# Grouped attention on one core: fresh tiles for score slots and output banks, other waits, and a plan with other constants

## The chip, the core and the metric

The kernel runs on one core of a Trainium2 chip. Five engines of the core take part, each with its own stream of instructions: TensorE (PE) multiplies matrices into PSUM, VectorE (DVE) and ScalarE (ACT) work on elements, GpSimd (POOL) and SyncE (SP) here mostly issue transfers (DMA). [...]The metric is device time of one execution in microseconds (us): 372.54 us before the change, the median of three runs (372.14 to 372.68).

## What is computed

Attention with 8 query heads that share 2 key/value heads in groups of four; batch 8, sequence 1024, head dimension 64:

```python
# q: (8, 8, 1024, 64), k and v: (8, 2, 1024, 64), all float32
for g in range(2):
    q_group = q[:, 4 * g : 4 * g + 4]          # four query heads of one group
    scores = (1 / sqrt(64)) * q_group @ k[:, g:g+1].transpose(0, 1, 3, 2)
    attn = exp(scores - max(scores, axis=-1))
    attn = attn / (sum(attn, axis=-1) + 1e-8)
    output[:, 4 * g : 4 * g + 4] = attn @ v[:, g:g+1]
```

The kernel calls one pair of batch and query head a job: 64 jobs. The 1024 keys of a job are cut into 8 chunks of 128 keys, so there are 512 chunks of scores of 128 x 1024 numbers each, each of which needs an exponential. The maximum is not subtracted (the scores are small); the sum of a row comes out of the second product, since v has a column of ones beside it.

## The kernel before

TensorE writes a chunk of scores into one of three slots in PSUM (`sps[0..2]`, two banks each). A slot is emptied in one of two ways. ScalarE takes most chunks, with one exponential each. VectorE takes about a quarter and builds an exponential out of bits: a first pass (`yt`, out of the slot) turns the score into a 16-bit integer that, read as bfloat16, is a power of two with a linear mantissa; three more operations, over two chunks at once, split it into two numbers `et` and `zt` whose sum is the exponential. The second product takes both, which makes two matmuls instead of one for each piece of such a chunk.

```python
elif kind == "score":
    for half in range(2):
        now = nc.tensor.matmul(sps[x][:, half, :], lhsT=..., rhs=..., start=True, stop=True)
elif kind == "act":
    p = pp.tile([128, 2, HS], BF16, name="pt")
    nc.scalar.activation(out=p, in_=sps[x], func=AF.Exp, scale=scale)
elif kind == "dpass":
    nc.vector.tensor_scalar(out=yt[ch][:, i, :, :], in0=sps[x], scalar1=EXP_A, scalar2=EXP_B,
                            op0=ALU.mult, op1=ALU.add)
# "zh":  zt = (yt & 0x7F) | 0x3F00      "two": et = yt & 0x7F80      "mul": zt = yt * zt
elif kind == "pv":        # second product into one of two output banks: 7 pieces of 128 rows per bank
    nc.tensor.matmul(ops[plan.group_of[x] % 2][...], lhsT=p[...], rhs=va[...], ...)
elif kind == "pvl":       # the same for the last job, chunk by chunk, into a score slot that is spare by then
    ...
elif kind in ("rec", "norm"):   # VectorE: reciprocal of the row sums, then multiply into ost
    ...
elif kind == "store":     # DMA of one job's 1024 rows out of ost, a ring of 56 pieces
    ...
```

In which order all this is issued is decided ahead of time, in Python, by a class `Plan`. It steps through the clocks of TensorE, ScalarE and VectorE with constants for the length of each operation and for the hand-over between engines, and writes down the list of events from which the instructions are then issued. A few of the constants (in ns) and the rule for a score that is meant for ScalarE:

```python
M_PAIR = 226      # the two score matmuls of a chunk
M_PTAIL = 45      # from there to the exponential that reads them
M_ACT = 905       # an exponential
M_GAP = 120; M_RUNWAY = 1300; M_BACK = 3000; M_WAIT = 150; GRAIN = 4
...
runway = tA - t + M_ACT * len(aq)
slack = runway - cold * M_PAIR - M_PTAIL - (M_SWITCH if mode != "s" else 0)
...
if slack <= M_GAP or (full and runway < M_RUNWAY):
    kind = "A"            # now a score for ScalarE; otherwise second products, GRAIN matmuls at a time
```

`M_BACK` is the amount of pending work under which VectorE is given another chunk. The tile framework puts in the semaphore waits from what each operation reads and writes. Each `sps[i]` and `ops[i]` is one tile for the whole kernel.

At the start, k and q of the first job are loaded as float32, cast, transposed by TensorE into slot 2 (k in its first half, q in its second) and copied out:

```python
nc.sync.dma_start(out=f32["k"], in_=rows(k[0, 0]))       # rows: "(c p two) d -> p c (two d)", 512-byte runs
nc.scalar.dma_start(out=f32["q"], in_=rows(q[0, 0]))
...
nc.vector.tensor_copy(out=k0[:, 0, 0:128], in_=turned["k"][:, 0:128])
nc.scalar.activation(out=qt[0][:, 0, 0:256], in_=turned["q"][:, 0:256], func=AF.Copy)
nc.vector.tensor_copy(out=qt[0][:, 0, 256:HS], in_=turned["q"][:, 256:HS])
nc.vector.tensor_copy(out=k0[:, 0, 128:HS], in_=turned["k"][:, 128:HS])
```

Of the kernel before, what the change touches and what calls it, by code (L numbers as in the profile page):

```python
# [9 lines left out]

M_START = 5150
M_SWAP = 700
M_Q1 = 3500
# [5 lines left out]
M_PAIR = 226  # L19
M_PTAIL = 45  # L20
M_SWITCH = 92
M_MM = 33.5
# [3 lines left out]
M_FIX = 76  # L26
# [5 lines left out]
M_REC = 115  # L32
M_GAP = 120
M_RUNWAY = 1300
M_BACK = 3000
M_WAIT = 150
STEP = 10
INF = float("inf")
PB = 7
NPIECE = 8  # L40
GRAIN = 4
MXD = 2
STEPS = (("zh", M_D4), ("two", M_D4), ("mul", M_D2))


class Plan:


    def __init__(self, nj, npt, nct, nyt):
        self.nj, self.npt, self.nct, self.nyt = nj, npt, nct, nyt  # L50
        self.ev = []
        self.on_d = set()
        self.spare = None
        self.mms = [8] * nj

        self.last = (nj - 1) * NPIECE
        self.groups = [(i, min(i + PB, self.last)) for i in range(0, self.last, PB)]
        self.groups += [(self.last, self.last + 4), (self.last + 4, self.last + 8)]
        self.group_of = [g for g, (lo, hi) in enumerate(self.groups) for _ in range(lo, hi)]
        self.run()  # L60

    def run(self):
# [3 lines left out]
        qready = [M_START] + [M_START + M_Q1 + M_QSTEP * j for j in range(nj - 1)]  # L66
        slot_free = [M_START, M_START, M_START + M_SWAP]
        aq, dq = [], []
# [14 lines left out]
        a = 0  # L83

        def pick_d():
            for j in range(a, min(nj, a + 3)):
                if todo[j] and dcount[j] < MXD and qready[j] <= tP:
                    return j
            if a == nj - 1 and len(todo[a]) > 2 and dcount[a] < MXD + 1:
                return a  # L90
            return None

        while pc < last or steps or norms:
# [12 lines left out]
            if tD == t:  # L106
                end = None
                if dq and dq[0][0] <= t:
                    _, s, j, c = dq.pop(0)
                    if open_chain is None:  # L110
                        open_chain = dict(id=nch, pairs=[], at=0)
                        ch_left[nch] = set()
                        nch += 1
                        used_c += 1
# [16 lines left out]
                else:  # L131
# [4 lines left out]
                    for ch in chains:  # L136

                        late = dlast == (ch["id"], 0) and ch["at"] == 0
                        key = (late, 3 - ch["at"], ch)
                        if best is None or key[:2] < best[:2]:  # L140
                            best = key
                    if best:
                        at = max(t, dend + M_DEP) if best[0] else t
                        ch = best[2]
                        if ch is None:
                            _, _, lo, hi = norms.pop(0)
                            ev.append((t, "norm", (lo, hi), None, None))
                            end = at + M_FIX + 64 * (hi - lo) * M_D1
                            out_free[group_of[lo] % 2] = end + M_DTAIL + M_SEE
                            dlast = None  # L150
                        else:
                            n = len(ch["pairs"])
                            kind, rate = STEPS[ch["at"]]
                            ev.append((t, kind, None, ch["id"], n))
                            end = at + M_FIX + 1024 * n * rate
                            ch["at"] += 1
                            dlast = (ch["id"], ch["at"])
                            if ch["at"] == len(STEPS):
                                chains.remove(ch)
                                for j, c in ch["pairs"]:  # L160
                                    p_ready[j][c] = end + M_DTAIL + M_SEE
# [12 lines left out]
            if not dq and len(chains) < self.nyt and (open_chain or used_c < self.nct):  # L174
                back = max(tD - t, 0)
                for ch in chains:
                    n = len(ch["pairs"])
                    back += sum(M_FIX + 1024 * n * r for _, r in STEPS[ch["at"] :])
                if back < M_BACK:
                    dj = pick_d()  # L180
# [11 lines left out]
            if kind:  # L192
# [13 lines left out]
                else:  # L206
                    dcount[j] += 1
                    self.mms[j] += 1
                    self.on_d.add((j, c))
            elif (  # L210
# [33 lines left out]
            elif (  # L244
# [14 lines left out]
                ev.append((tP, "pvl", c, len(steps), None))  # L259
                tP += NPIECE * M_MM * (2 if (nj - 1, c) in self.on_d else 1)  # L260
                if not steps:
# [18 lines left out]
def kernel(  # L280
# [42 lines left out]
    rp = ctx.enter_context(tc.tile_pool(name="rp", bufs=4))  # L323
    psum = ctx.enter_context(tc.tile_pool(name="psum", bufs=1, space=bass.MemoryType.PSUM))

    ctx.enter_context(tc.manual_schedule())

    sps = [psum.tile([128, 2, HS], FP32, name=f"sp{i}") for i in range(3)]
    ops = [psum.tile([128, 512], FP32, name=f"ops{i}") for i in range(2)]
    RING = PB * NPIECE  # L330
# [17 lines left out]
    def cast_k(b, g):  # L348
# [5 lines left out]
        )  # L354

    def load_v(b, g):
        t = vsp.tile([128, NH, 2 * D], FP32, name="vs")
        vs[(b, g)] = t
        return nc.sync.dma_start(
            out=t, in_=v[b, g].rearrange("(c p two) d -> p c (two d)", p=128, two=2)  # L360
        )

# [28 lines left out]

    def rows(x):
        return x.rearrange("(c p two) d -> p c (two d)", p=128, two=2)

    f32 = {x: kvp.tile([128, NH, 2 * D], FP32, name=f"{x}32") for x in "kq"}
    b16 = {x: kvp.tile([128, NH, 2 * D], BF16, name=f"{x}16") for x in "kq"}
    kt[(0, 0)] = ktp.tile([128, 2, HS], BF16, name="kt")
    qt[0] = qp.tile([128, 1, HS], BF16, name="qt")
    nc.sync.dma_start(out=f32["k"], in_=rows(k[0, 0]))
    nc.scalar.dma_start(out=f32["q"], in_=rows(q[0, 0]))  # L400
    load_v(0, 0)
    cast_q(1)
    make_identity(nc, ident)
    cast_q(2)

    def dummy(n, cols):
# [7 lines left out]
    nc.scalar.activation(out=b16["q"], in_=f32["q"], func=AF.Copy)  # L414
    turned = {"k": sps[2][:, 0, :], "q": sps[2][:, 1, :]}
    for x in "kq":
# [13 lines left out]
    nc.vector.tensor_copy(out=k0[:, 0, 0:128], in_=turned["k"][:, 0:128])  # L430
    nc.scalar.activation(out=qt[0][:, 0, 0:256], in_=turned["q"][:, 0:256], func=AF.Copy)
    nc.vector.tensor_copy(out=qt[0][:, 0, 256:HS], in_=turned["q"][:, 256:HS])  # L432
    nc.vector.tensor_copy(out=k0[:, 0, 128:HS], in_=turned["k"][:, 128:HS])
# [29 lines left out]
    pt, yt, et, zt, where = {}, {}, {}, {}, {}  # L463
    now = None

    def terms(j, par):

        for ci in range(NC):
            c = ci if par == 0 else (ci + NH) % NC
            if (j, c) in where:  # L470
                ch, i = where[(j, c)]
                yield ci, et[ch].bitcast(BF16)[:, i, par, :]
                yield ci, zt[ch].bitcast(BF16)[:, i, par, :]
            elif (j, c) in pt:
                yield ci, pt[(j, c)][:, par, :]

    for _, kind, x, j, c in ev:
        if kind in ("ck", "cq"):
# [13 lines left out]
        elif kind == "score":  # L492
            b, h = divmod(j, H)
            t = kt[(b, h // HPG)]

            for half in range(2):
# [9 lines left out]
        elif kind == "act":  # L506
            p = pp.tile([128, 2, HS], BF16, name="pt")
            pt[(j, c)] = p
            nc.scalar.activation(out=p, in_=sps[x], func=AF.Exp, scale=scale)  # L509
        elif kind == "dpass":  # L510
            ch, i = j
            where[c] = j
            if i == 0:
                yt[ch] = yp.tile([128, 2, 2, HS], U16, name="yt")
            nc.vector.tensor_scalar(  # L515
                out=yt[ch][:, i, :, :], in0=sps[x],
                scalar1=EXP_A, scalar2=EXP_B, op0=ALU.mult, op1=ALU.add,
# [8 lines left out]
        elif kind == "two":  # L526

            et[j] = ep.tile([128, 2, 2, HS], U16, name="et")
            nc.vector.tensor_scalar(  # L529
                out=et[j][:, 0:c], in0=yt[j][:, 0:c], scalar1=0x7F80, scalar2=None,  # L530
                op0=ALU.bitwise_and,
            )
        elif kind == "mul":
            z = zt[j].bitcast(BF16)[:, 0:c]
            nc.vector.tensor_tensor(  # L535
                out=z, in0=yt[j].bitcast(BF16)[:, 0:c], in1=z, op=ALU.mult
            )
        elif kind == "pv":
# [3 lines left out]
            lo = x % PB * (D + 1)  # L542
            every = list(terms(job, par))
            for i in range(j, j + c):
                ci, p = every[i]
# [9 lines left out]
        elif kind == "pvl":  # L555
            b, h = divmod(NJ - 1, H)
            first = j == NC - 1
            for i in range(NPIECE):
                par = i % 2
# [13 lines left out]
        elif kind == "half":  # L573
# [3 lines left out]
            (nc.scalar if i else nc.sync).dma_start(  # L577
                out=out[b, h].rearrange("(s p two) d -> p s (two d)", p=128, two=2)[:, i : i + 2],
                in_=ost[:, lo % RING : lo % RING + 4, :].rearrange("p (s two) d -> p s (two d)", two=2),
# [19 lines left out]
        elif kind == "store":  # L599
            b, h = divmod(j, H)  # L600
            r = j * NPIECE % RING
            nc.sync.dma_start(
                out=out[b, h].rearrange("(s p two) d -> p s (two d)", p=128, two=2),
                in_=ost[:, r : r + NPIECE, :].rearrange("p (s two) d -> p s (two d)", two=2),
            )


# [28 lines left out]
```

## Time and profile before

| what | us |
|---|---|
| time, median of 3 | 372.54 |
| span of the profiled execution, first to last instruction | 370.2 |
| first exponential starts | 7.95 |
| last exponential starts / ends | 362.23 / 363.26 |
| last matmul ends | 366.04 |
| ScalarE, VectorE, TensorE busy | 356.5, 354.1, 349.7 |

A line of a group reads: line of the kernel, engine, operation, what it writes and reads with shapes, count; then busy time and the mean length of one in ns; then the idle time of the engine just ahead of these operations, and who ended it. Busy time counts overlapping records once. A line of the timeline reads: start and length in us, engine, line, operation, count, and in brackets the idle time ahead of it and who ended that. A line of the table of waits reads: who waited for whom, us in total, how often, the longest.

### The profile page before, as it was taken

To read this page: it belongs to the slowest core of one execution; us is meant where nothing else is said; L and a number is where in the kernel's file an instruction comes from. 1 tells how busy PE (TensorE), PEld (TensorE's weight loads), DVE (VectorE), ACT (ScalarE), POOL (GpSimd) and SP (SyncE) were. 2 spreads that over 40 slices of the span, in tenths; PEclk is the share of its full clock that TensorE was granted. 3 is DMA by queue.
4 is the path that set the end of the run, shared out by engine and by line. 5 is a ranking of instruction groups with operands and counts; after the bars stand their busy time and mean duration, and the time that the engine had idled before them with its cause. 6 is when DMAs were issued, how large, how long until landed. Compare 5 with 4: busy or idle time off the path is not lost.

```text
span 370.2 us, 14248 instructions
## 1 busy us (share of the span) xinstructions
PE 349.7 (94%) x6199; PEld 222.7 (60%) x6199; DVE 354.1 (96%) x479; ACT 356.5 (96%) x386; POOL 50.6 (14%) x100
## 2 busy tenths in 40 slices
PE   6899999999999999999999999999999999999995
PEld 2465666666565666666566666656666656666655
DVE  3999999999999999999999999999999999999995
ACT  3999999999999999999999999999999999999992
POOL 4002021011212011021111112102011111201000
PEclk9999999999999999999999999999999999999999
DMA  7446756865757674776566577466576756775223
GB/s 178 78 88 106 157 121 101 151 136 130 125 113 132 118 159 86 147 139 120 104 140 133 122 133 119 114 158 115 107 154 96 155 97 143 122 143 98 60 58 87
DMA packets 90702, 44.83 MB, mean 121 GB/s; under 512 B 45488, under 2 KB 89392, under 8 KB 89392
## 3 DMA queue, kind: packets, MB, share of 16 engines
q1 hardware_dynamic: 87344, 33.31, 39.1%
q0 software_dynamic: 2496, 10.23, 20.5%
q8 instruction: 48, 0.79, 1.0%
q10 hardware_dynamic: 800, 0.39, 0.4%
q14 instruction: 14, 0.11, 0.2%
HBM read 25.17 MB, written 27.00 MB: 141 GB/s over the span
## 4 chain that ended last, share of the span: by engine, by line
ACT 39%; DVE 24%; PE 24%; issue 10%; DMA 2%; DVEq 0%; ACTq 0%
ACT pt L509 39%; DVE yt L515 13%; PE ops L546 12%; PE sp L499 11%; DVE zt L535 4%; DVE zt L522 2%; DVE et L529 2%; DVE ost L593 2%; DMA qt<-qd 1%; DMA k<-in_k_dram 1%; PE sp L565 1%; DVE rec L590 1%; PE sp L418 0%; DVE k L413 0%; DVE qt L432 0%
## 5 line engine op out<-in xcount | busy, mean ns | idle before, releaser
L509 ACT ACTIVATE pt<-sp 128x1024 bf16<-128x1024 f32 x383 | 354.2, 1054 | 2.2 <-PE sp L499 1.6
L499 PE MATMUL sp<-qt,kt 64*128 64x512 bf16 x1024 | 172.0, 384 | 13.3 <-ACT pt L509 6.2
L546 PE MATMUL ops<-va,pt 128*128 128x65 bf16 x3024 | 176.8, 194 | 0.0
L515 DVE TENSOR_SCALAR yt<-sp 128x1024 uint16<-128x1024 f32 x129 | 157.1, 1218 | 6.1 <-PE sp L499 4.8
L546 PEld LDWEIGHTS <-pt 128*128 128x128 bf16 x3024 | 129.2, 97 | 52.6 <-issue 52.6
L546 PE MATMUL ops<-va,et 128*128 128x65 bf16 x1008 | 120.4, 194 | 0.0
L546 PE MATMUL ops<-va,zt 128*128 128x65 bf16 x1008 | 119.5, 194 | 0.9 <-DVE zt L535 0.6
L546 PEld LDWEIGHTS <-et 128*128 128x128 bf16 x1008 | 79.6, 98 | 28.4 <-issue 26.2
L546 PEld LDWEIGHTS <-zt 128*128 128x128 bf16 x1008 | 80.3, 97 | 2.4 <-DVE zt L535 1.5
L535 DVE TENSOR_TENSOR zt<-yt,zt 128x2048 bf16<-128x2048 bf16 (+1 forms) x65 | 80.5, 1238 | 0.0
L499 PEld LDWEIGHTS <-kt 64*128 64x128 bf16 x1024 | 47.9, 93 | 53.4 <-issue 31.7
L343 POOL DMA_DIRECT2D qd<-in_q_dram x63 | 32.9, 522 | 223.8 <-PE sp L499 212.8
L529 DVE TENSOR_SCALAR et<-yt 128x2048 uint16<-128x2048 uint16 (+1 forms) x65 | 44.8, 690 | 0.0
L593 DVE TENSOR_TENSOR ost<-ops,rec 128x448 f32<-128x448 f32 x72 | 44.2, 614 | 0.0
L522 DVE TENSOR_SCALAR zt<-yt 128x2048 uint16<-128x2048 uint16 (+1 forms) x65 | 44.0, 677 | 0.0
L351 POOL DMA_DIRECT2D kd<-in_k_dram x15 | 7.3, 488 | 59.4 <-PE sp L499 51.2
L590 DVE RECIPROCAL rec<-ops 128x7 f32<-128x7 f32 x72 | 14.1, 196 | 0.0
L364 POOL CAST va<-vs 128x512 bf16<-128x512 f32 x16 | 10.2, 638 | 2.4 <-DMA vs<-in_v_dram 2.4
L408 PE MATMUL ops<-warm 128*128 128x128 bf16 (+1 forms) x31 | 5.0, 308 | 1.2 <-DVE warm L335 1.2
L408 PEld LDWEIGHTS <-warm 128*128 128x128 bf16 x31 | 2.2, 108 | 4.2 <-issue 3.0
L413 DVE CAST k<-k 128x512 bf16<-128x512 f32 x1 | 0.4, 429 | 2.6 <-DMA k<-in_k_dram 2.6
L414 ACT ACTIVATE q<-q 128x512 bf16<-128x512 f32 x1 | 0.6, 629 | 2.2 <-DMA q<-in_q_dram 2.2
(28 smaller groups left out, 18.6 us busy)
## 6 DMA issues: line engine op xcount, KB each, us to landing
out_dram<-ost SPq DMA_DIRECT2D x63, 256.0 KB, 2.8
qd<-in_q_dram POOLq DMA_DIRECT2D x63, 128.0 KB, 3.5
vs<-in_v_dram SPq DMA_DIRECT2D x16, 256.0 KB, 4.2
kd<-in_k_dram POOLq DMA_DIRECT2D x15, 128.0 KB, 3.2
kt<-kt SPq DMA_DIRECT2D x30, 64.0 KB, 3.6
qt<-qd SPq DMA_TRANSPOSE x63, 3.8
k<-in_k_dram SPq DMA_DIRECT2D x1, 256.0 KB, 3.6
q<-in_q_dram ACTq DMA_DIRECT2D x1, 256.0 KB, 4.0
```

Source lines behind the costliest of these rows:

```text
L343: return nc.gpsimd.dma_start(out=t.rearrange("(a x) d -> a (x d)", x=4), in_=q[b, h].rearrange("(a x) d -> a (x d)", x=8),)
L351: return nc.gpsimd.dma_start(out=t.rearrange("(a x) d -> a (x d)", x=4), in_=k[b, g].rearrange("(a x) d -> a (x d)", x=8),)
L364: return nc.gpsimd.tensor_copy(out=va[:, b * G + g, :, :, 0:D], in_=vs.pop((b, g)).rearrange("p c (two d) -> p c two d", two=2),)
L499: now = nc.tensor.matmul(sps[x][:, half, :], lhsT=t[lo : lo + D, c // NH, ci % NH * 128 : (ci % NH + 1) * 128], rhs=qt[j][lo : lo + D, 0, ...
L509: nc.scalar.activation(out=p, in_=sps[x], func=AF.Exp, scale=scale)
L515: nc.vector.tensor_scalar(out=yt[ch][:, i, :, :], in0=sps[x], scalar1=EXP_A, scalar2=EXP_B, op0=ALU.mult, op1=ALU.add,)
L522: nc.vector.tensor_scalar(out=zt[j][:, 0:c], in0=yt[j][:, 0:c], scalar1=0x7F, scalar2=0x3F00, op0=ALU.bitwise_and, op1=ALU.bitwise_or,)
L529: nc.vector.tensor_scalar(out=et[j][:, 0:c], in0=yt[j][:, 0:c], scalar1=0x7F80, scalar2=None, op0=ALU.bitwise_and,)
L535: nc.vector.tensor_tensor(out=z, in0=yt[j].bitcast(BF16)[:, 0:c], in1=z, op=ALU.mult)
L546: nc.tensor.matmul(ops[plan.group_of[x] % 2][:, lo : lo + D + 1], lhsT=p[:, qs * 128 : (qs + 1) * 128], rhs=va[:, b * G + h // HPG, ci % N ...
L590: nc.vector.reciprocal(out=rec[:, 0:n], in_=o[:, :, D])
L593: nc.vector.tensor_tensor(out=ost[:, r : r + n, :], in0=o[:, :, 0:D], in1=rec[:, 0:n].unsqueeze(2).to_broadcast([128, n, D]), op=ALU.mult,)
```

## The change

It does six things. Each use of a score slot and of an output bank becomes a tile of its own, in a pool with one buffer per slot, so that the readers of the slot's earlier contents are waited for by the matmul that writes, and no longer by the operation that reads. Every twelfth exponential is made to depend on the one fifteen before it, so that the others need no wait on their own engine for a buffer written long before. Waits for old stores are put on one of VectorE's three short operations (`two`) and not on the normalisation. The plan's constants are changed, among them the hand-over from scores to their reader (`M_PTAIL`). For the last two jobs VectorE adds `et` and `zt` itself, and the second product takes one matmul per piece. The first k, q and v are loaded, and the first output stored, with runs of 2 KB (another order of the rows, the same for all four), and q is transposed into slot 1 and copied out in one piece.

```diff
-M_START = 5150
-M_SWAP = 700
+M_START = 5450
+M_SWAP = 1200
-M_PTAIL = 45
+M_PTAIL = 205
-M_GAP = 120
-M_RUNWAY = 1300
-M_BACK = 3000
-M_WAIT = 150
+M_GAP = 60
+M_RUNWAY = 1500
+M_BACK = 2500
+M_WAIT = 200
-GRAIN = 4
+GRAIN = 3
-STEPS = (("zh", M_D4), ("two", M_D4), ("mul", M_D2))
+TAIL = 2
+STEPS = (("zh", M_D4), ("two", M_D4), ("mul", M_D2), ("add", M_D2))
... (in the plan: jobs from nj - TAIL on have the fourth step, and no second matmul;
...  the last job's third chunk for VectorE, allowed before, is gone)
-    psum = ctx.enter_context(tc.tile_pool(name="psum", bufs=1, space=bass.MemoryType.PSUM))
+    banks = {
+        x: ctx.enter_context(tc.tile_pool(name=x, bufs=1, space=bass.MemoryType.PSUM))
+        for x in ("sp0", "sp1", "sp2", "op0", "op1")
+    }
-    sps = [psum.tile([128, 2, HS], FP32, name=f"sp{i}") for i in range(3)]
-    ops = [psum.tile([128, 512], FP32, name=f"ops{i}") for i in range(2)]
+    def new_slot(i):
+        sps[i] = banks[f"sp{i}"].tile([128, 2, HS], FP32, name=f"sp{i}")
+        return sps[i]
... (new_bank likewise)
+    def rows(x, fours=False):
+        how = "(p c two) d -> p c (two d)" if fours else "(c p two) d -> p c (two d)"
-    nc.sync.dma_start(out=f32["k"], in_=rows(k[0, 0]))
-    nc.scalar.dma_start(out=f32["q"], in_=rows(q[0, 0]))
+    nc.sync.dma_start(out=f32["k"], in_=rows(k[0, 0], True))
+    nc.scalar.dma_start(out=f32["q"], in_=rows(q[0, 0], True))
-    turned = {"k": sps[2][:, 0, :], "q": sps[2][:, 1, :]}
+    turned = {"k": new_slot(2)[:, 0, :], "q": new_slot(1)[:, 0, :]}
-    nc.scalar.activation(out=qt[0][:, 0, 0:256], in_=turned["q"][:, 0:256], func=AF.Copy)
-    nc.vector.tensor_copy(out=qt[0][:, 0, 256:HS], in_=turned["q"][:, 256:HS])
+    nc.scalar.activation(out=qt[0][:, 0, :], in_=turned["q"], func=AF.Copy)
... (score)
+            where_s[(j, c)] = new_slot(x)
... (act; the first pass likewise reads where_s)
-            nc.scalar.activation(out=p, in_=sps[x], func=AF.Exp, scale=scale)
+            exps.append(nc.scalar.activation(out=p, in_=where_s[(j, c)], func=AF.Exp, scale=scale))
+            if len(exps) % 12 == 0 and len(exps) > 16:
+                tc.add_manual_dep(
+                    exps[-1].ins, exps[-16].ins.name, Sync, reason="buffers written before"
+                )
... (two)
+            while stores and stores[0][0] < when - 10000:
+                tc.add_manual_dep(ins.ins, stores.pop(0)[1].ins.name, Sync, reason="old stores")
+        elif kind == "add":
+            z = zt[j].bitcast(BF16)[:, 0:c]
+            nc.vector.tensor_tensor(
+                out=z, in0=et[j].bitcast(BF16)[:, 0:c], in1=z, op=ALU.add
+            )
```

## The prediction

> **What bounds the kernel now.** I read the page's busy line first, then the costliest groups, the table of waits, and the timeline of the first 8 us and the last 8 us; what the views round away I took from the start and end times of single records of the trace.
>
> The busy line says that no engine is alone at the limit:
>
> ```profile
> PE 349.7 (94%) x6199; PEld 222.7 (60%) x6199; DVE 354.1 (96%) x479; ACT 356.5 (96%) x386; POOL 50.6 (14%) x100
> ```
>
> ScalarE and VectorE both stand at 96%, so a gain has to be had on both. The groups say with what they are filled:
>
> ```profile
> L509 ACT ACTIVATE pt<-sp 128x1024 bf16<-128x1024 f32 x383 | 354.2, 1054 | 2.2 <-PE sp L499 1.6
> L499 PE MATMUL sp<-qt,kt 64*128 64x512 bf16 x1024 | 172.0, 384 | 13.3 <-ACT pt L509 6.2
> L515 DVE TENSOR_SCALAR yt<-sp 128x1024 uint16<-128x1024 f32 x129 | 157.1, 1218 | 6.1 <-PE sp L499 4.8
> ```
>
> 512 score chunks: 383 exponentials on ScalarE, 129 first passes on VectorE. Idle time before the exponentials is only 2.2 us, and that misleads. The records of neighbours overlap (mean 1054 ns, but a new one starts every 904 ns, the median of the 382 distances from start to start), so an exponential that comes 100 or 200 ns late leaves no gap; it only shrinks the overlap. The count shows it: from the first start (7.95 us) to the last (362.23 us) are 354.28 us, and 382 x 0.904 is 345.3 us. So 8.9 us are lost there, a third of it at most visible as a wait. Of these, 7.6 us sit in 67 distances of more than 925 ns, and most of the rest in the exponential after each late one, which typically starts 17 ns later than 904.
>
> Whom the 67 wait for I got by pairing each with its two score matmuls. In all but two the slot had been free for over 100 ns (median 0.36 us) when the scores were started, so TensorE was busy with other work: they were issued too late, not held up by the slot. The exponential starts 428 ns (median) after the start of the second score matmul in the 11 cases where it carries one wait, and 489 ns in the 56 where it carries two. The second wait thus costs some 60 ns, though it is on something long finished.
>
> VectorE shows the same, and here as idle time:
>
> ```profile
> DVE yt L515 <- PE sp L499: 4.8, 15, 0.7
> ```
>
> 32 of its first passes start with over 20 ns of idle time before them, 6.0 us in all; 27 of the 32 carry two waits and start 496 ns after the second score matmul, 5 carry one and start at 419.
>
> The start and the end are the third part:
>
> ```profile
> 4.35 0.43 DVE L413 CAST k<-k 128x512 bf16<-128x512 f32 x1 [2.64 <-DMA k<-in_k_dram]
> 4.75 0.63 ACT L414 ACTIVATE q<-q 128x512 bf16<-128x512 f32 x1 [2.22 <-DMA q<-in_q_dram]
> ...
> 6.41 0.38 ACT L431 ACTIVATE qt<-sp 128x256 bf16<-128x256 f32 x1 [1.03 <-DVE kt L430]
> 6.83 0.42 DVE L432 CAST qt<-sp 128x256 bf16<-128x256 f32 x1 [0.45 <-ACT qt L431]
> ```
>
> ```profile
> 366.13 0.18 DVE L590 RECIPROCAL rec<-sp 128x4 f32<-128x4 f32 x1 [1.31 <-PE sp L565]
> ```
>
> The loads of k and q end the first waits; then q's transpose leaves in two halves one behind the other (6.41 to 7.25 us), the second half on VectorE. At the end the last exponential ends at 363.26 and the last VectorE multiplication at 364.04, but the last 88 matmuls (L565) run until 366.04; two normalisations and the store make it 370.2.
>
> **What the Trainium skill says.** Perfetto Trace Analysis, Identifying Dependency Chains: an instruction that waits for several engines may get EventSemaphore instructions in front of it. The trace agrees, with 279 of them before the exponentials and 68 before the first passes:
>
> ```profile
> L509 ACTq EVENT_SEMAPHORE  x279: 17/17/840, 8.0 to 362.0; - x140
> L515 DVEq EVENT_SEMAPHORE  x68: 21/21/21, 15.9 to 359.1; - x68
> ```
>
> VectorE: DVE Perf Modes, The DRAIN you can't avoid: a semaphore after each operation cost nothing extra there. That agrees for waits already met: the normalisations (L593) with a store's wait in front overlap their predecessor by about 83 ns, those without by about 82. So a wait only costs where its instruction is late. DMA: Bandwidth & Descriptors, Why small descriptors are slow: each DMA operation carries a fixed metadata cost, so fewer and larger pieces are better. The trace of before has 512-byte pieces only in these first loads (27 ns each on its engine); what 2 KB pieces take, no run here shows yet.
>
> **The change part by part.** What is on each engine I counted in the two programs' instruction orders.
>
> *Waits.* Fresh tiles drop the wait for the slot's last reader: 70 exponentials lose a VectorE wait, 68 first passes a ScalarE wait. Self-waits of exponentials fall from 226 to 31. On ScalarE the late ones gain 56 x 60 ns = 3.4 us, capped by how late each was: 7.6 falls to 4.5 us. On VectorE 27 x 77 ns = 2.1 us. The store waits leave the 56 normalisations for 51 operations that mostly had no wait: worth about nothing, by the 83 against 82 ns above.
>
> *Plan.* The hand-over constant grows by 160 ns (45 to 205; with the 226 that the plan counts for a pair this is 431, near the 428 measured), the margin falls by 60: a score for ScalarE is started some 100 ns earlier before it runs dry. Taking 100 ns more off each of the 67 leaves about 1.3 us of the 4.5, with 17 still late. With their followers, and new late ones in a denser plan, I put the loss on ScalarE at 2.5 us instead of 8.9: **-6.4 us**. For VectorE I take 6.0 to about 2.5: -3.5 us.
>
> *Split.* 384 exponentials and 128 first passes: +0.9 us on ScalarE. VectorE loses one pass of 1.14 us and the three short operations of a single chunk (0.34 + 0.34 + 0.60): -2.4 us. Its two adds over 128x2048 cost what the same-sized multiplication does, 1.14 us from start to start: +2.3 us. TensorE loses 40 of 5128 products of probabilities with values, some 1.2 us at about 30 ns, of use only at the end.
>
> *Start.* The 2 KB loads: k landed 3.6 us after issue, q 4.0. 512 pieces at 27 ns over 16 engines are 0.86 us; I guess 0.4 us less for both. q's transpose leaves in one ScalarE operation, which need no longer wait for VectorE's read of the shared slot: 6.1 to 6.75 instead of 6.41 to 7.25 (0.63 us is the 512-wide operation of L414): 0.5 us. First score and first exponential **-0.9 us**.
>
> *End.* In the new order the last job has 64 products, not 88, and behind the last exponential's wait stand 8, some 0.25 us; in before the last product ended 2.8 us behind the last exponential. If VectorE is ready by then: **-2.3 us**. It probably is not far off: before, its last multiplication ended 0.8 us behind the last exponential. From the items above it comes forward by 0.9 + 3.5 + 2.4 - 2.3 = 4.5, to 359.5 us with its last add. In the new order one normalisation more stands behind this add than stood behind the last multiplication (0.53 us from start to start), so 359.0. ScalarE's last exponential: 363.3 - 0.9 + 0.9 - 6.4 = 356.9.
>
> *Sum.* By ScalarE, with 0.4 us to the last product, 1.3 for the normalisations and 2.9 for the store: 356.9 + 4.6 = 361.5. By VectorE: 359.0, then up to 48 products (1.4 us, those that the order puts from the add's chunks on), 1.3 and 2.9: 364.6. The executions took 372.54 against a span of 370.2, so +2.3: 363.8 by one and 366.9 by the other. VectorE's figure rests on the more cautious guess (3.5 of 6.0 us), and the order places the add's products three chunks ahead of the last exponential's, as if the add were done by then, so I lean to ScalarE's and say **364.3 us**, 2.2% less.
>
> **Rivals.** (1) *Latency bound by slots*: with three slots and the score started as soon as it can be, the ring exponential, score, exponential becomes the limit, and earlier issue can't help. Against it: 65 of the 67 late scores found a slot already free; for it: the group of score matmuls shows 6.2 us waiting for ScalarE. Then only the 60 ns count: about 366.8. (2) *VectorE becomes the bound*: its dependent operations keep their stalls and the backlog limit shrinks from 3.0 to 2.5 us, so it may run dry more often. For it: 6.0 us idle today, and the two adds are dependent chains at the very end. About 366 to 368. (3) *Almost no wait left*: waits fall to about 1 us on both, the loads gain 1 us: about 361.5. (4) *TensorE becomes the bound*: 94% busy overlaps itself, and idle time before its scores is 13.3 us, so I give it little; then 368 or more.
>
> **Range and chances.** Rivals 1 and 2 set the upper end, 3 the lower: 361.0 to 367.8. The 2% line is at 365.1, 0.8 us above my number, with an uncertainty of about 2.5 us: **0.6 faster, 0.38 within 2%, 0.02 slower**. All parts point the same way, and slower would need a plan that misses by 14 us.
>
> **What would show it.** Right: EVENT_SEMAPHORE before the exponentials near 31 and before the first passes 0; first exponential near 7.05 us; mean distance of exponentials from 927 to about 911 ns; late ones at 428 ns behind their second score, none at 489; last product within 0.5 us of the last exponential. Wrong: as many late exponentials as before with the slot just released (rival 1); VectorE idle still at 6 us, or L605 waiting for the add at the end (rival 2); k landing no sooner than 3.6 us.

## The result, and the profile after

| what | before | after |
|---|---|---|
| time, median | 372.6 us | 366.81 us (366.55 to 367.96) |
| span of the profiled execution | 370.2 us | 364.9 us |
| exponentials on ScalarE | 383 | 384 |
| first exponential starts | 7.95 us | 7.36 us |
| last exponential ends | 363.26 us | 360.28 us |
| last product ends | 366.03 us | 360.76 us |
| last VectorE operation of a chunk ends | 364.04 us | 356.62 us |

The change makes the kernel faster by 1.5%: ratio 0.9853, 95% interval 0.9831 to 0.9876. That lies inside the range, but the gain is smaller than the 2.2% that I had put in the middle: I had given 0.6 to a gain of more than 2% and 0.38 to one within 2%, and it was within.

The page of after, its busy line and the two groups that empty the slots (in a group: busy time, mean length of one in ns, then idle time ahead of them):

```profile
PE 346.3 (95%) x6155; PEld 220.5 (60%) x6155; DVE 351.6 (96%) x476; ACT 355.1 (97%) x387; POOL 51.3 (14%) x100
...
L532 ACT ACTIVATE pt<-sp 128x1024 bf16<-128x1024 f32 x384 | 352.6, 1099 | 1.0 <-PE sp L522 0.7
...
L543 DVE TENSOR_SCALAR yt<-sp 128x1024 uint16<-128x1024 f32 x128 | 155.8, 1217 | 2.3 <-PE sp L522 2.1
```

Divide busy time by count: 352.6 / 384 = 918 ns for one exponential, where before it was 354.2 / 383 = 925. Records of this group overlap and busy time counts them once. A late exponential that leaves no gap stays in this busy time, so the quotient is the pace plus the delays that the overlap hides, an upper limit of the pace. The distance from one end to the next shows the pace itself: its median is 917 ns in before and in after. The idle time ahead of VectorE's first passes fell from 6.1 to 2.3 us. The waits themselves, counted at the operations, are those that the change was to remove; the first passes have no line of this kind any more:

```profile
L532 ACTq EVENT_SEMAPHORE  x31: 17/17/17, 28.4 to 358.2; - x31
```

The start, from the timeline of after (start and length in us):

```profile
4.33 0.63 ACT L434 ACTIVATE q<-q 128x512 bf16<-128x512 f32 x1 [1.89 <-DMA q<-in_q_dram]
4.51 0.43 DVE L433 CAST k<-k 128x512 bf16<-128x512 f32 x1 [2.80 <-DMA k<-in_k_dram]
...
6.07 0.60 ACT L451 ACTIVATE qt<-sp 128x512 bf16<-128x512 f32 x1 [1.10 <-PE sp L438]
...
7.36 3.99 ACT L532 ACTIVATE pt<-sp 128x1024 bf16<-128x1024 f32 x4 [0.70 <-PE sp L522]
```

q's cast comes 0.42 us sooner than before, k's 0.16 us later; q's copy is one operation and ends at 6.67 us instead of 7.25. The end, VectorE's timeline of after:

```profile
355.39 1.23 DVE L571 TENSOR_TENSOR zt<-et,zt 128x2048 bf16<-128x2048 bf16 x1
356.53 0.62 DVE L633 TENSOR_TENSOR ost<-ops,rec 128x448 f32<-128x448 f32 x1
358.49 0.21 DVE L630 RECIPROCAL rec<-ops 128x7 f32<-128x7 f32 x1 [1.33 <-PE ops L584]
358.73 0.62 DVE L633 TENSOR_TENSOR ost<-ops,rec 128x448 f32<-128x448 f32 x1
360.80 0.18 DVE L630 RECIPROCAL rec<-sp 128x4 f32<-128x4 f32 x1 [1.45 <-PE sp L605]
```

The last add ends at 356.62 us, 3.66 us ahead of the last exponential, and after that VectorE waits for TensorE. Of the two engines that empty the slots, ScalarE is the one that sets the end.

**The ledger of the span.** The parts below are differences of the times in the table and of the count of exponentials; the lost time of ScalarE is the time from the end of the first exponential to the end of the last, less 917 ns for each after the first (why 917 and not the 904 of the prediction is the first experiment):

| part | before | after | difference, us |
|---|---|---|---|
| start of the first exponential | 7.95 | 7.36 | -0.59 |
| the exponentials, 383 and 384: the first 1.02, each other 0.917 | 351.32 | 352.24 | +0.92 |
| lost time between exponentials | 3.99 | 0.68 | -3.31 |
| last exponential to last product | 2.77 | 0.48 | -2.29 |
| last product to the end of the span | 4.17 | 4.11 | -0.06 |
| sum | 370.2 | 364.9 | -5.33 |

### The profile page after: what moved, and what is told of

The parts are those of the page before. It is cut to its first block, busy times and chain, and to the rows that moved or that the text cites. A ratio compares the mean times of both kernels' runs of the same rounds, so it can differ in the third digit from the quotient of the medians.

```text
span 364.9 us, 13795 instructions
## 1 busy us (share of the span) xinstructions
PE 346.3 (95%) x6155; PEld 220.5 (60%) x6155; DVE 351.6 (96%) x476; ACT 355.1 (97%) x387; POOL 51.3 (14%) x100
## 3 DMA queue, kind: packets, MB, share of 16 engines
q0 software_dynamic: 2496, 10.23, 21.3%
## 4 chain that ended last, share of the span: by engine, by line
ACT 56%; DVE 37%; PE 4%; DMA 1%; issue 1%
ACT pt L532 56%; DVE yt L543 16%; DVE zt L566 8%; DVE zt L550 5%; DVE ost L633 4%; DVE et L557 4%; PE sp L522 2%; DMA k<-in_k_dram 1%; DVE rec L630 1%; PE ops L584 1%; PE sp L605 1%; PE sp L438 0%; PE ops L428 0%; ACT qt L451 0%; DVE k L433 0%
## 5 line engine op out<-in xcount | busy, mean ns | idle before, releaser
L532 ACT ACTIVATE pt<-sp 128x1024 bf16<-128x1024 f32 x384 | 352.6, 1099 | 1.0 <-PE sp L522 0.7
L584 PE MATMUL ops<-va,pt 128*128 128x65 bf16 x3024 | 184.6, 194 | 0.0
L584 PEld LDWEIGHTS <-pt 128*128 128x128 bf16 x3024 | 135.9, 97 | 43.2 <-issue 43.2
L584 PE MATMUL ops<-va,zt 128*128 128x65 bf16 x1008 | 124.5, 194 | 0.0
L584 PEld LDWEIGHTS <-zt 128*128 128x128 bf16 x1008 | 83.2, 97 | 6.9 <-issue 6.9
L566 DVE TENSOR_TENSOR zt<-yt,zt 128x2048 bf16<-128x2048 bf16 x64 | 78.0, 1220 | 0.0
L550 DVE TENSOR_SCALAR zt<-yt 128x2048 uint16<-128x2048 uint16 x64 | 46.4, 724 | 0.1
L557 DVE TENSOR_SCALAR et<-yt 128x2048 uint16<-128x2048 uint16 x64 | 43.2, 676 | 0.0
```

Of the source, the lines that this page charges most:

```text
L532: exps.append(nc.scalar.activation(out=p, in_=where_s[(j, c)], func=AF.Exp, scale=scale))
L550: nc.vector.tensor_scalar(out=zt[j][:, 0:c], in0=yt[j][:, 0:c], scalar1=0x7F, scalar2=0x3F00, op0=ALU.bitwise_and, op1=ALU.bitwise_or,)
L557: ins = nc.vector.tensor_scalar(out=et[j][:, 0:c], in0=yt[j][:, 0:c], scalar1=0x7F80, scalar2=None, op0=ALU.bitwise_and,)
L566: nc.vector.tensor_tensor(out=z, in0=yt[j].bitcast(BF16)[:, 0:c], in1=z, op=ALU.mult)
L584: nc.tensor.matmul(ops[plan.group_of[x] % 2][:, lo : lo + D + 1], lhsT=p[:, qs * 128 : (qs + 1) * 128], rhs=va[:, b * G + h // HPG, ci % N ...
```

## The experiments

Each experiment has its own measurements of before beside it, with medians of 372.3 or 372.8 us. Ratios to before are therefore the better comparison between experiments; that of after is 0.9853 (0.9831 to 0.9876), and 0.001 of it is 0.37 us.

Two theories of the lost time stand against each other. Theory A: ScalarE's pace is that at which exponentials end; a start every 904 ns only runs ahead of it and takes up part of a late start. Theory B is the prediction's: 904 ns is the pace, and every later start is lost.

### The pace by itself

The kernel leaves the attention out: 76 exponentials of the same shape out of one PSUM tile into tiles of their own, then zeros as the output.

```diff
+    N1, N2, N3 = 44, 16, 16
... (dv and po: memsets on VectorE and GpSimd, issued ahead of the loop)
+    for i in range(N1 + N2 + N3):
+        p = pp.tile([128, 2, S // 2], BF16, name="pt")
+        e = nc.scalar.activation(out=p, in_=sp, func=AF.Exp, scale=1.0 / math.sqrt(D))
+        if i >= N1:
+            tc.add_manual_dep(e.ins, dv[i - N1].ins.name, Sync, reason="one met wait")
+        if i >= N1 + N2:
+            tc.add_manual_dep(e.ins, po[i - N1 - N2].ins.name, Sync, reason="two met waits")
```

> A kernel that leaves the attention out (its output is zeros): 76 exponentials of 128x1024 out of one PSUM tile, one after the other, into tiles of their own, nothing else running beside them after the first microseconds; the first 44 without a wait, 16 with one wait that was met long before, 16 with two. Theory A (the pace of ScalarE is that of the ends, 917 ns; a start every 904 ns only runs ahead of it): ends 917 apart in all three parts, and the lead of the starts grows by 13 ns each until something stops it. Theory B (my prediction's: 904 ns is the pace): ends come to 904 apart when no other engine is at work. Met waits: by both theories 0 ns, since a wait costs only where the instruction is late; the rival, that a second wait costs its 17 to 60 ns each time, makes the last part 934 to 977 apart.

In run e1 ends were 916.6 ns apart in the first part, 916.7 in the second and 916.7 in the third; starts were 904 to 905 ns apart in all three. The group, and ScalarE's timeline of this kernel:

```profile
L41 ACT ACTIVATE pt<-sp 128x1024 bf16<-128x1024 f32 x76 | 69.8, 1474 | 0.0
```

```profile
2.03 69.77 ACT L41 ACTIVATE pt<-sp 128x1024 bf16<-128x1024 f32 x76
```

The mean record is 1474 ns long, and the last one 1942: each start runs some 12 ns further ahead of its end than the one before, and nothing stopped that in 76. But 69.77 us for 76, less the 1.025 us of the first, is 916.6 ns for each of the 75 others. The stores of the zeros, which I had not reckoned with in the expectation, kept the DMA engines busy for most of the run; the last part ran on past their end at the same pace. So theory A holds: 917 ns is the pace, with no other engine at work on it. And a wait that was met long before costs nothing here, one or two of them. Here is also the limit of what this run shows: the 16 EVENT_SEMAPHOREs of the last part ran at 46.2 to 59.9 us, their exponentials started at 56.3 to 69.9 us, so these waits were dealt with some 10 us ahead.

With this the records of before read otherwise. Only 54 exponentials end more than 920 ns after the one before (4.2 us over 917 ns in all), 49 of them with two waits; the whole loss is 3.99 us, and not the 8.9 that I had taken. After has 9 such exponentials and a loss of 0.68 us. Four of the 9 carry two waits and start at 487 to 489 ns; they are twelfth ones, which keep the dependency.

### The thinned self-waits, undone in after and done alone in before

```diff
 after, without:
-            if len(exps) % 12 == 0 and len(exps) > 16:
-                tc.add_manual_dep(
-                    exps[-1].ins, exps[-16].ins.name, Sync, reason="buffers written before"
-                )
 before, with the same four lines added and nothing else
```

> After, without the dependency of every twelfth exponential: 235 exponentials carry a second wait on ScalarE itself instead of 31; all else, the order too, is the same. Theory A: only exponentials whose scores leave less than 61 ns to spare become late; from the records of after these are 13, with 0.6 us in all, so +0.5 to +1.0 us. Theory B (every late start counts, by 61 ns): some 40 of the 47 late ones, about +2.3 us. Rival, waits are free: 0.

Run e2 measured 367.27 us, ratio to before 0.9869 (0.9853 to 0.9886). In the trace 17 exponentials end late instead of 9, 15 of them with two waits (14 of these start 488 to 490 ns after their second score matmul), and the loss is 1.12 us instead of 0.68. The two kernels are 0.46 us apart by the medians and 0.6 by the ratios, at the lower edge of theory A's band; the two intervals overlap, so it is the trace that carries this.

> Before, with that dependency alone added: exponentials with two or more waits fall from 279 to 93, the order stays. Theory A: by the records of before, 39 exponentials that end late lose a wait and gain up to 61 ns each, 1.7 us in all: 370.9. Theory B, with 56 late starts: 3 us, 369.5. Rival, waits are free: 372.6.

Run e3 measured 371.06 us, ratio 0.9961 (0.9948 to 0.9975): clearly faster than before, by 1.2 us by the medians and 1.5 by the ratio. The loss went from 3.99 to 3.15 us, the late ends from 54 to 35, and those with two waits from 49 to 11; the ones that stayed late now mostly start at 428 to 430 ns. The last exponential and VectorE's last chunk both end 0.8 us sooner, and so does the span. The interval, 0.9 to 1.9 us, takes in theory A's 1.7 us and excludes B's 3. That the trace shows 0.8 us only has a reason at the start, apart from the waits. In all but one of the profiled executions the first score matmuls last 579 to 632 ns, and from some time on 372 to 387. In before that change comes between 10.1 and 11.2 us, in this execution between 12.6 and 13.7, and its fifth exponential ends 0.71 us late; in before the fifth is not late. After the 15th exponential the loss fell from 3.85 to 2.38 us, by 1.5.

### The plan of before in after

```diff
-M_START = 5450; M_SWAP = 1200; M_PTAIL = 205; M_GAP = 60; M_RUNWAY = 1500; M_BACK = 2500; M_WAIT = 200; GRAIN = 3
+M_START = 5150; M_SWAP = 700; M_PTAIL = 45; M_GAP = 120; M_RUNWAY = 1300; M_BACK = 3000; M_WAIT = 150; GRAIN = 4
... (put on one line here; the plan's first time for the third slot goes back too)
```

> After, with the plan's constants of before (hand-over 45, margin 120 and the rest), all else as after. Theory A: with the thinned waits the order of before leaves about 1.5 us of late ends on ScalarE where after has 0.7, and VectorE waits some 4 us where after has 2.3: +1 us, at most +2. Theory B: late starts of 4.5 us where the new plan should leave 1.3: +3 us.

Run e4 measured 368.04 us, ratio 0.9885 (0.9871 to 0.9898): 1.2 us slower than after. The loss is 2.23 us (28 late ends) instead of 0.68, the last exponential ends at 361.29, and VectorE's last chunk only at 360.70 us, 0.6 us ahead of it and not 3.7. Its idle time shows in the group of this kernel:

```profile
L543 DVE TENSOR_SCALAR yt<-sp 128x1024 uint16<-128x1024 f32 x128 | 155.8, 1217 | 4.4 <-PE sp L522 3.5
```

4.4 us instead of 2.3. So the new plan is worth 1.2 us, in the band of theory A and far from B's 3. In the profiled executions the difference of the loss is larger, 1.55 us, but in this one the score matmuls took 372 to 387 ns from the first on, and the first exponential started at 6.83 us, 0.54 us sooner than in after.

### The end: no adds, and a third chunk for VectorE

```diff
-TAIL = 2
+TAIL = 0
 and for the second kernel also, as before has it:
+            if a == nj - 1 and len(todo[a]) > 2 and dcount[a] < MXD + 1:
+                return a
```

> After, with TAIL = 0: no adds, two matmuls again for the pieces of the last two jobs that VectorE made (80 products of the last job instead of 64, and behind the last scores 100 matmuls instead of 69, some 0.9 us more at 30 ns). If the adds shorten the end: the last scores start some 2.4 us ahead of the end of the last exponential, 92 matmuls that don't need it take 2.8 us, so the last product comes 0.4 to 0.9 us later, 367.2 to 367.7. Rival, the end is bound by the last exponential alone and VectorE had 3.7 us to spare: no difference, 366.8.

Run e5 measured 367.35 us, ratio 0.9850 (0.9836 to 0.9863). By the time this can't be told from after. In the trace the last product ends 1.11 us behind the last exponential instead of 0.48, as the count of products says, so the adds do shorten the end by 0.6 us in the profiled execution; that the time gains as much is not shown.

> After, with TAIL = 0 and with the rule of before that lets VectorE have a third chunk of the last job: 383 exponentials, 88 products of the last job, VectorE's last chunk alone at the very end, as before. If the end of before (2.8 us from the last exponential to the last product) came from this third chunk and its doubled products: one exponential less (-0.9) and 1 to 2 us more at the end than e5, 367.5 to 368.5. Rival, the end of before came from the late plan on VectorE alone: 366.0 to 366.8.

Run e6 measured 368.81 us, ratio 0.9890 (0.9877 to 0.9904), a little slower than I expected. ScalarE, with one exponential less, loses 1.98 us instead of 0.69 in e5. But 1.30 us of this are lost in two exponentials that end at 19.8 and 21.3 us: the TensorE clock granted in this execution is 0.5 from 16.5 to 20.0 us, and 1.0 there in e5 and in after. The rest, 0.68 us, is that of e5, so this delay says nothing of the end. The last product is 2.26 us behind the last exponential. VectorE's timeline at the end of this kernel:

```profile
358.71 0.68 DVE L568 TENSOR_TENSOR zt<-yt,zt 128x1024 bf16<-128x1024 bf16 x1
360.63 0.20 DVE L632 RECIPROCAL rec<-ops 128x7 f32<-128x7 f32 x1 [1.23 <-PE ops L586]
...
363.35 0.18 DVE L632 RECIPROCAL rec<-sp 128x4 f32<-128x4 f32 x1 [1.86 <-PE sp L607]
```

VectorE is done with its last chunk at 359.39 us and then waits for TensorE twice; the order has put 27 products of the second-last job and all 88 of the last one behind the last scores. Of the 2.3 us that the end gained, then, the larger part (1.15 us, 2.26 against 1.11) goes with the third chunk of the last job, which is ScalarE's again, and 0.6 us with the adds; the 0.5 us that are left, to 2.77, no run took apart. The 1.15 us are paid for with the exponential that ScalarE has more, 0.92 us, so this part of the change is worth some 0.2 us on balance.

### The start: q's copy and the loads

```diff
 first kernel:
-    turned = {"k": new_slot(2)[:, 0, :], "q": new_slot(1)[:, 0, :]}
-    nc.scalar.activation(out=qt[0][:, 0, :], in_=turned["q"], func=AF.Copy)
+    new_slot(2)
+    turned = {"k": sps[2][:, 0, :], "q": sps[2][:, 1, :]}
+    nc.scalar.activation(out=qt[0][:, 0, 0:256], in_=turned["q"][:, 0:256], func=AF.Copy)
+    nc.vector.tensor_copy(out=qt[0][:, 0, 256:HS], in_=turned["q"][:, 256:HS])
 second kernel, also for q, v and the first store:
-    nc.sync.dma_start(out=f32["k"], in_=rows(k[0, 0], True))
+    nc.sync.dma_start(out=f32["k"], in_=rows(k[0, 0]))
```

> After, with q transposed into the second half of slot 2 and copied out in two halves, by ScalarE and then VectorE. By the two timelines of the start the first exponential moved 7.95 to 7.36 us; if this came from the copy: 7.9 again and +0.5 us, 367.3. Rival, it came from the loads: no difference, 366.8.

Run e7 measured 367.81 us, ratio 0.9867 (0.9853 to 0.9880): 1.0 us slower than after by the medians, 0.5 by the ratios. The first exponential starts at 7.98 us, and the reason stands in its timeline:

```profile
6.44 0.38 ACT L452 ACTIVATE qt<-sp 128x256 bf16<-128x256 f32 x1 [1.07 <-DVE kt L451]
6.86 0.42 DVE L453 CAST qt<-sp 128x256 bf16<-128x256 f32 x1 [0.45 <-ACT qt L452]
```

ScalarE waits for VectorE's read of k out of the same slot, then VectorE for ScalarE. One copy out of a slot of its own takes both waits away. How much that gives, the next run shows better: the first exponential also moves with the landing of the loads and the length of the first matmuls, and in the nine executions with after's copy and loads it starts between 6.83 and 7.75 us.

> After, with 512-byte runs in the first loads of k, q and v and in the first store. k landed 3.6 us after its issue before and 3.7 after, q 4.0 and 3.6. k is needed first, so by the copy theory nothing is gained by 2 KB: first exponential within 0.2 us of 7.36, 366.6 to 367.0. By my prediction's: 0.4 us later, 367.2.

Run e8 measured 366.77 us, ratio 0.9838 (0.9825 to 0.9852), and the first exponential at 7.38 us. Its issue lines and those of after, one below the other (KB each, us from issue to landing):

```profile
k<-in_k_dram SPq DMA_DIRECT2D x1, 256.0 KB, 3.6
q<-in_q_dram ACTq DMA_DIRECT2D x1, 256.0 KB, 4.0
```

```profile
q<-in_q_dram ACTq DMA_DIRECT2D x1, 256.0 KB, 3.6
k<-in_k_dram SPq DMA_DIRECT2D x1, 256.0 KB, 3.7
```

In after the 2 KB loads bring q 0.4 us sooner and k 0.1 later, and k is needed first: they gain nothing. Other executions agree: with 2 KB k landed after 3.5 to 4.1 us and q after 3.6 to 4.0 (ten executions), with 512 bytes after 3.6 and 4.0 (three). A 2 KB piece takes 84 ns on its DMA engine and a 512-byte piece 27, so that 256 KB over 16 engines need 0.67 us instead of 0.86. In e8 both loads landed as in before, and the first exponential came 0.57 us sooner (7.38 against 7.95): that is the worth of q's copy.

### The fresh tiles

```diff
     def new_slot(i):
-        sps[i] = banks[f"sp{i}"].tile([128, 2, HS], FP32, name=f"sp{i}")
+        if sps[i] is None:
+            sps[i] = banks[f"sp{i}"].tile([128, 2, HS], FP32, name=f"sp{i}")
         return sps[i]
 (new_bank likewise)
```

> After, with one tile per score slot and output bank for the whole kernel again; the dependency of every twelfth exponential stays. Exponentials with two waits or more go from 31 to 84 and first passes from 0 to 55. By theory A and the records of after none of the exponentials that get a wait has less than 61 ns to spare, and VectorE has time to spare: 366.8, at most +0.4. By my prediction the fresh tiles give VectorE 2.1 us, some of it on the path: +0.5 to +2.

Run e12 measured 366.88 us, ratio 0.9845 (0.9824 to 0.9866): no difference in the time, whose two intervals would hide up to some 1 us. In the trace ScalarE's loss is 0.47 us, VectorE's idle time ahead of its first passes 2.5 us instead of 2.3, and its last add ends at 356.63 us, as in after. On top of the plan and the thinned self-waits the fresh tiles bring nothing that these runs can see. What they bring to the kernel of before was not tried by itself.

### A plan with the measured pace, and less for ScalarE

```diff
-M_ACT = 905
+M_ACT = 917
 second kernel also (third: j in (20, 42)):
-                if todo[j] and dcount[j] < MXD and qready[j] <= tP:
+                if todo[j] and dcount[j] < MXD + (j in (31,)) and qready[j] <= tP:
```

> After, with the plan's constant for an exponential at 917 ns, the pace of the ends, instead of 905; 384 exponentials as before. Theory A: ScalarE in after loses only 0.7 us over 917 ns each, so a plan that knows the pace can win at most that: 366.2 to 367.0. Theory B: the plan now starts scores later than they are needed by the pace of 904, so more exponentials come late: 367.5 or more.

Run e9 measured 367.43 us, ratio 0.9858 (0.9845 to 0.9872): no gain. By the median this lies between the bands of both theories and nearer to B's 367.5, by the ratio 0.2 us above after, so the time does not decide between them. In the trace 11 exponentials end late instead of 9; the loss is 1.04 us instead of 0.68, 0.49 of it in one exponential at 254 us, and the last product is 0.71 us behind the last exponential.

> As e9, and VectorE may take a third chunk of one job in the middle: 383 exponentials and 129 first passes. If after is bound by ScalarE's pace, one exponential less is worth 0.92 us: 365.7 to 366.0, as VectorE, which needs 2.35 us more, had 3.7 us to spare at its end. Rival, VectorE or TensorE has no room in the middle: no gain, 366.8 or more.

Run e10 measured 365.57 us, ratio 0.9801 (0.9787 to 0.9816), whose interval lies below that of after: the best version, 1.2 us under it by the medians and 1.9 by the ratios. ScalarE has 383 exponentials, loses 0.46 us, and ends at 359.21 us; VectorE is done with its last add at 356.32.

> As e10 with a third chunk in two jobs: 382 exponentials, 130 first passes. VectorE needs 4.7 us more than in after, where 3.7 were to spare at the end and 2.3 in waits. If that fits: 364.9 to 365.3. If VectorE becomes the bound, as I expect: later last add than last exponential, 366 to 367.

Run e11 measured 367.31 us, ratio 0.9855 (0.9841 to 0.9868). ScalarE loses 1.53 us and ends at 359.44 us, later than in e10 with one exponential less, and VectorE is late too, as its timeline shows:

```profile
359.31 1.22 DVE L571 TENSOR_TENSOR zt<-et,zt 128x2048 bf16<-128x2048 bf16 x1
360.45 0.62 DVE L633 TENSOR_TENSOR ost<-ops,rec 128x448 f32<-128x448 f32 x1
361.29 0.18 DVE L630 RECIPROCAL rec<-sp 128x4 f32<-128x4 f32 x1 [0.23 <-PE sp L605]
```

The last add ends at 360.53 us, 1.09 us behind the last exponential, and the products that need it end at 361.25. In these places the room on VectorE was good for one chunk and not for two; whether two chunks in other jobs would fit was not tried.

## Why the prediction was right, and where it was wrong

The number was inside the range and the direction right, but it was 2.5 us too low, and the term that was mis-sized can be named.

**The lost time on ScalarE (wrong in size, right in kind).** The prediction said "382 x 0.904 is 345.3 us. So 8.9 us are lost there" and put 2.5 us in its place, -6.4 us. The term was mis-sized because 904 ns, the median distance of the starts, was taken as the pace. At 917 ns the loss was 3.99 us, of which the change took 3.31; it left 0.68 us, less than the 2.5 that I had allowed. The profile of before held the warning: mean records of 1054 ns, while an exponential that starts with no lead takes 1017 to 1026, mean that starts were running ahead of ends. In the Trainium skill, ScalarE: Activation LUTs, What ACT_TABLE_LOAD costs, gives 186 ns + 0.833 ns for each element less an overlap of some 93 ns, from which I estimate 946 ns. The traces do not agree: the run's 917 lies between this estimate and 904, and it decides.

**The late ones and the second wait (right).** Late exponentials with two waits mostly start at 487 to 490 ns, those with one mostly at 427 to 430, in before, in after and in the experiments; so the 60 ns stand. "A wait only costs where its instruction is late" agrees with the 32 exponentials with met waits at an unchanged pace. But "capped by how late each was" was applied to late starts, not to late ends, which made 3.4 us out of what was 0.5 to 0.6 us when undone in after and 1.2 to 1.5 us when done alone in before. Of the late starts in after, 47 by the prediction's measure and not 17, all but 9 are taken up by the lead and cost nothing.

**The plan (right in kind, too large).** It gives 1.2 us. VectorE's idle time fell to 2.3 us (the prediction: "about 2.5"); with the old plan it is 4.4 us. The 2.1 us that the prediction gave to the fresh tiles on VectorE did not show: without them it is 2.5 us, under the new plan.

**The split (right).** One exponential more for +0.92; the experiment with 383 gave back 1.9 us against e9, whose plan has the same constants. By the two traces 0.92 of that is the exponential and 0.58 a smaller loss.

**The start (half right).** -0.59 instead of -0.9: q's copy gave 0.57, the "0.4 us less for both" of the loads nothing, because k, which comes first, did not land sooner.

**The end (right in size, open in part).** -2.29 against "-2.3". That the two agree so closely is partly luck: the runs account for 1.75 us, by the last job's products and the adds, and not for the other 0.5. The add ended at 356.6 and not at 359.0, so the figure by VectorE, 364.6, was too cautious, and the lean towards ScalarE's was right.

**From span to time.** "+2.3" set the median time against the span of another execution; the profiled executions, 371.99 and 366.65 us, are 1.8 us above their own spans. That made the number 0.5 us too high. In all, for ScalarE's path: 361.5, + 3.1 for the lost time (3.31 instead of 6.4), + 0.3 for the start, is 364.9, the measured span. With 1.8 us more it is the profiled 366.65; of its 2.4 us above 364.3, then, 3.4 are these two terms, less 0.5 for the "+2.3" and 0.5 for the lean from 363.8 up to 364.3.

**The rivals.** Slots as the bound: no; all 9 late ends of after found their slot free for 359 ns or more. That this rival's 366.8 us is the measured number is chance. VectorE as the bound: not in after, but with two chunks more. Almost no wait left: in kind this came closest, since ScalarE's lost time did fall below 1 us; what it lacked was that the pace itself was longer. TensorE as the bound: in after its lateness can have cost no more than the 0.68 us between exponentials and the 0.48 at the end; it was not tried by itself.

**The signs.** As foretold there are 31 EVENT_SEMAPHOREs before the exponentials and none before the first passes, and the last product is within 0.5 us. The mean distance of starts is 918 ns and not 911, and nine of the 47 late starts still stand at 487 to 489 ns. Two readings were off without weight for the number: of the five first passes with one wait three start at 418 to 419 ns and two, before 11 us, at 641 and 646; and the 2% line for slower, 380 us, is 15.7 us from 364.3, not 14.

## What to carry to other kernels

Take the pace of an engine whose records overlap from the distance of their ends (the median, where some are late), and only then work out what is lost; busy time divided by count is an upper limit (925 ns in before, at a pace of 917), since late ones hide in it; a late start that the engine's backlog takes up costs nothing. Once an engine runs at that pace without gaps, better waits and plans are worth no more: give it fewer operations, as long as the next engine still ends ahead of it. Where the work goes matters: a chunk for VectorE in the last job cost 1.15 us at the end and saved 0.92, one in the middle was part of the best version. A second wait, on something long finished, was free on exponentials that were not waiting for anything else, and cost some 60 ns on those whose real wait had only just ended. Half a microsecond at the start is not to be read from a single trace, as the range of 6.83 to 7.75 us above shows.

## What the runs showed of the hardware that was not expected

- Records of back-to-back exponentials start every 904 ns and end every 917 ns. Over 76 of them without a gap the lead of the starts grew from 1.02 to 1.94 us and did not stop; the first after a late one begins again at 1.02.
- 32 exponentials with one or two waits that were met before did not change this pace (916.7 against 916.6 ns). The semaphore instructions of the last 16 ran some 10 us ahead of their exponentials.
- The first score matmuls last 579 to 632 ns and later ones 372 to 387. The change came after the last of these long ones at 7.6 (e9) to 12.6 us (e3), in e4 ahead of the first score at 6.4 us.
- In one execution (e6) the granted TensorE clock was 0.5 from 16.5 to 20.0 us, and ScalarE, which waited for TensorE's scores, lost 1.30 us there.
- 256 KB loaded in runs of 2 KB landed after 3.5 to 4.1 us (k) and 3.6 to 4.0 us (q) in ten executions, in runs of 512 bytes after 3.6 and 4.0 us in three.
